# A hybrid layer's delta-rule heads: silu of k in a batch of its own, z projected behind the silu of the rest

## Chip, cores and metric

The kernel runs on one core of a Trainium2 chip. The metric is device microseconds of one execution; three executions of the kernel before are at hand, and one execution has a profile. In the rows PE is TensorE (PEld its weight loads), DVE is VectorE, ACT is ScalarE, POOL is GpSimd and SP is SyncE, which issues most DMAs.

## What is computed

One layer over 1024 tokens and 1024 channels, all in float32. The part that matters here is branch A, eight heads of a bidirectional gated delta rule:

```
h = rmsnorm(x);  proj = h @ w_in                         # q, k, v, z of 8 heads x 128 channels, and more
q, k, v = split(silu(centred_conv5(proj_qkv)))           # convolution of 5 taps along the tokens
q, k = l2norm(q), l2norm(k)
o = delta_rule(q, k, v, decay_f, beta_f) + flip(delta_rule(flip(q, k, v), decay_b, beta_b))
y_a = (rmsnorm(o) * w * silu(z)) @ w_proj_gdn
# branch B: gated linear attention, 4 heads; then gates, a merge, an output projection and a norm
```

## The kernel before

Every product with a weight is made in three matmuls from exact float32r pairs (hi·hi, hi·lo, lo·hi). A block of 128 projected channels (`project`) takes 48 matmuls of 512 columns. Its weight comes in two halves, and each half is loaded by SP (`raw`, two buffers), rounded by ACT (`hi`) and reduced to its rest by POOL (`lo`). `next_w` loads up to four halves ahead of the one that is used. ACT copies the two PSUM banks of a block out: into a padded tile `xp` for k, q and v (three buffers), into `gz` and from there to DRAM (`z_d`) for z.

A head h of branch A goes through these steps:

- `gdn_project`: k, q, v are projected in this order; each is convolved by DVE (five operations of 128x1024, for q the first is ACT's). In the kernel before, the heads from 1 on then project z, load the z of the head before (`zs`, one buffer), and only then run one batch of silu: a load of ACT's silu table, silu of q, k, v and the head before's z, and a load of the table that holds exp and ln. Head 0 has k's silu in a batch of its own already.
- `gdn_decay`: the decays `dt` of 16 units, by small matmuls into the banks `pd`, an exp on ACT (L588) and a mask on POOL (L570).
- `gdn_inverse`: k is transposed into `pk` (L603), ACT copies it and takes its squares, `um` is formed (L629), then inverted: substitution in blocks of 32 on DVE (L652, L654), and blocks of 64 and 128 on PE (L683 to L718). It ends with a ln and an exp on ACT (L724) and the tiles that the scan needs.
- `gdn_scan`: eight steps, both directions side by side, each a chain of PE, DVE and ACT (`r`, `vd`, `vn`, `S`, `po`).

The tiles of q, k, v, `dt`, `um` and `ktok` have two buffers each, so that head h + 2 takes those of head h. The banks of `pd` are those of the scan's `po`.

The order on each engine is made by a planner: every instruction has a place (`cur_priority`), and of those that are ready the one with the lowest place comes first. `gdn_inverse` of the next head stands ahead of `gdn_scan` of this one; projections have the place `P_FILL`, so they fill what the others leave. The result is a fixed queue for each engine. `keep_in_program_order` ties an instruction behind the one emitted just before it on its engine, so the table load of the batch comes behind z's last copy out of PSUM, and each silu behind the one before. Where a queue would run a function whose table is not loaded, a load is put in automatically. The last head has 13 blocks of another projection, the merge gates (`pj_t`), as filling; branch B follows.

Of the kernel before, what the change touches and what calls it, by code (L numbers as in the profile page):

```python
# [14 lines left out]
T = 1024  # L15
# [17 lines left out]
# tiles of loaded weights, of their split parts, of x normalised, of padded projections  # L33
WRAW, WSPLIT, XS, XP = 2, 4, 4, 3
# the order in which a head's k, q and v are projected
A_ORDER = (1, 0, 2)
# the tiles of x that GpSimd scales, the weights whose low parts it takes
X_POOL = (1, 3, 5, 7)
LO_POOL = "azqv"
# blocks of the first projection's gates that are loaded ahead, and the head after whose states  # L40
GA_AHEAD, GA_HEAD = 2, 2
# gates computed beside a head's scan
# [6 lines left out]
# places in the schedule's order  # L49
# [8 lines left out]
def const_array():  # L58
    """Masks and the like: they depend on shapes alone."""
    import numpy as np  # L60

    k = np.arange(P)[:, None]
    i = np.arange(P)[None, :]
    f = lambda m: m.astype(np.float32)
    parts = {}
    parts["ident"] = f(k == i)
    parts["iu"] = f(k <= i)
    parts["il"] = f(k >= i)
    parts["su"] = f(k > i)
    parts["sl"] = f(k < i)  # L70
    cf = np.where(i >= 64, f((k >= 64) & (k <= i)), -f((k > i) & (k <= 63)))
    cb = np.where(i < 64, f((k >= i) & (k <= 63)), -f((k >= 64) & (k < i)))
    lo, hi = f(k <= 63), f(k >= 64)
    parts["cf"] = np.concatenate([cf, lo[:, :1], hi[:, :1]], 1) / 16.0
    parts["cb"] = np.concatenate([cb, hi[:, :1], lo[:, :1]], 1) / 16.0
    p = np.arange(P)
    half = (p % 32) // 16
    r = np.arange(32)[None, :, None]
    s = np.arange(16)[None, None, :]
    parts["yinit"] = f(r == 2 * s + half[:, None, None]).reshape(P, 512)  # L80
    off = 0
    for n, a in parts.items():
        CONSTS[n] = (off, a.shape[1])
        off += a.shape[1]
    return np.ascontiguousarray(np.concatenate(list(parts.values()), 1), dtype=np.float32)
# [3 lines left out]
def layer_kernel(  # L89
# [23 lines left out]
    @contextmanager  # L113
    def at(priority):
        """what is emitted here comes in the schedule's order from this place on"""
        before = tc.cur_priority
        tc.cur_priority = priority
        yield
        tc.cur_priority = before
# [16 lines left out]
    def mm3(ps, lh, ll, rh, rl, n):  # L136
        """ps = (lh + ll)^T (rh + rl), summed over n pieces, without ll^T rl, which is
        below float32's last place."""
        steps = [(a, b, k) for k in range(n) for a, b in ((lh, rh), (lh, rl), (ll, rh))]
        for s, (a, b, k) in enumerate(steps):  # L140
            nc.tensor.matmul(ps, lhsT=a(k), rhs=b(k), start=(s == 0), stop=(s == len(steps) - 1))  # L141

    # ------------------------------------------------------------ what lives throughout
# [16 lines left out]
    # ------------------------------------------------------------ split weights, projections  # L160
    def split(src, hi, lo):
        """src as a float32r pair whose sum is exact"""
        nc.scalar.copy(hi, src)
        nc.vector.tensor_tensor(lo, src, hi.bitcast(F32), op=ALU.subtract)

    def load_w(src, cols, name, g):
        """part of the rows of columns of a weight, [p, k, n], 512 elements of a partition;
        cols: list of (first column, width, place)."""
        n = sum(w for _, w, _ in cols)
        kn = 512 // n  # L170
        raw = wpool.tile([P, kn, n], F32, tag="wraw", name=f"raw_{name}_{g}", bufs=WRAW)
        v = src.rearrange("(k p) n -> p k n", p=P)[:, g * kn:(g + 1) * kn]
        for c, w, to in cols:
            nc.sync.dma_start(raw[:, :, to:to + w], v[:, :, c:c + w])
        hi = wpool.tile([P, kn, n], F32R, tag="whi", name=f"hi_{name}_{g}", bufs=WSPLIT)
        lo = wpool.tile([P, kn, n], F32R, tag="wlo", name=f"lo_{name}_{g}", bufs=WSPLIT)
        i = nc.scalar.copy(hi, raw)  # L177
        if name == "sm":
            tc.keep_in_program_order(i)
        if name[0] in LO_POOL:  # L180
            nc.gpsimd.tensor_tensor(lo, raw, hi.bitcast(F32), op=ALU.subtract)  # L181
        else:
            nc.vector.tensor_tensor(lo, raw, hi.bitcast(F32), op=ALU.subtract)  # L183
        return hi, lo

    # the weights' blocks in the order of their use: parts of them are loaded ahead
# [41 lines left out]
    def project_tokens(name, th, evac):  # L228
        """src^T w for half of the tokens: evac(b, psum) takes [128 tokens, (2 chunks, 256)]"""
        ps = [bank(pj, "pj", f"pj_{name}_{b}") for b in range(2)]  # L230
        for g in range(4):
            hi, lo = next_w(name, g)
            for b in range(2):
                for c in range(2):
                    ts = slice((2 * b + c) * P, (2 * b + c + 1) * P)
                    for k in range(2):
                        kk = 2 * g + k
                        for i, (a, w) in enumerate(((hh, hi), (hl, hi), (hh, lo))):
                            # the first product in a bank clears its marks of what is written
# [6 lines left out]
    def piece(ps, hi, lo, src, th, g, kn, cols=slice(0, 512)):  # L246
        """ps += what the g-th kn pieces of the rows bring, for columns of half of the tokens"""
# [7 lines left out]
    def project(name, evac, src=None):  # L255
        """rows of w^T src: evac(th, psum) takes [channels, 512 tokens]"""
# [8 lines left out]
    def in_steps(name, ps, gn):  # L265
        """as project, by quarters of the tokens"""
# [8 lines left out]
    def project_out(name, dst):  # L275
        """a block of channels kept in DRAM"""
# [13 lines left out]
    # ------------------------------------------------------------ constants of the two mixers  # L290
# [23 lines left out]
    def exp_ln_table():  # L314
        """after a function of another table: the one that has both exp and ln"""
        table(EXP_LN)
# [3 lines left out]
    # ------------------------------------------------------------ h = rmsnorm(x), transposed  # L320
    with tc.tile_pool(name="xpool", bufs=2) as xpool:
# [23 lines left out]
        def scaled(t):  # L345
            """a tile of x normalised, its transpose"""
# [53 lines left out]
    # ------------------------------------------------------------ decays and gates of the scans  # L400
# [6 lines left out]
    def scan_gates(pool):  # L407
# [17 lines left out]
        # [tokens, direction, head, chunk]  # L425
# [19 lines left out]
        # exp of: the sums up to a token, of what is left of the chunk, of the whole chunk  # L445
# [15 lines left out]
    def finish(o_ps, wcol, rs, zs, o, dst, kc):  # L461
        """o * w * rs * zs, to its place in DRAM; zs is overwritten"""
# [5 lines left out]
    def rs_of(sq, pair, lhsT, eps, name, banks):  # L468
        """sq becomes (mean of sq over the channels + eps) ** -0.5; pair: room for sq as a float32r pair"""
# [11 lines left out]
    # ------------------------------------------------------------ gated delta rule  # L481
# [5 lines left out]
    def gdn_project(h, pool):  # L487
        a = [pool.tile([P, T], F32, tag=f"a{j}", name=f"{'qkv'[j]}{h}", bufs=2) for j in range(3)]
        silu = lambda t: tc.keep_in_program_order(nc.scalar.activation(t, t, AF.Silu))
        for j in A_ORDER:  # L490
# [18 lines left out]
            if h == 0 and j == A_ORDER[0]:  # L509
                table(SILU)  # L510
                silu(a[j])
                exp_ln_table()
# [8 lines left out]
        project_out(f"z{h}", z_d[:, h])  # L521
        zs[h - 1] = gdn_z(h - 1, pool)
        table(SILU)
        for t in a + [zs[h - 1]]:
            silu(t)
        exp_ln_table()
        return a
# [3 lines left out]
    def gla_stacks(pool):  # L531
        """(r, 1) and (w2, b2) as float32r pairs, stacked for (r_hi + r_lo)^T (w_hi + w_lo) without
        r_lo^T w_lo, with the other direction's columns zero"""
# [32 lines left out]
    def causal(out, src, d, n):  # L566
        """src where the token of the partition is not after (d = 0) or not before (d = 1)
        that of the column, else 0"""
# [4 lines left out]
    def gdn_decay(h, pool):  # L573
        """dt[j, u, i] = exp(sum of lg over the tokens after j, up to i)"""
# [17 lines left out]
    def gdn_inverse(h, pool, sm, qkv, dt):  # L592
        qT, kT, vT = qkv
        t2 = lambda n, shape: pool.tile(shape, F32, tag="t2", name=f"{n}{h}", bufs=4)
        # keys and values by tokens, norms of the keys
# [22 lines left out]
        # um[j, unit, i] = (k_j . k_i) c1_j dt  # L618
# [13 lines left out]
        # um becomes (1 + um)^-1: blocks of 32 by substitution, all units at once  # L632
# [30 lines left out]
        # forward: yq = y, xq = y^T; backward: the other way round  # L663
# [6 lines left out]
        # blocks of 64, then of 128  # L670
# [55 lines left out]
        # values times the keys' norms, dt times k_j . q_i  # L726
# [17 lines left out]
    def gdn_scan(h, pool, sm, qkv, dt, um, ktok, vtok, c1, c2):  # L744
# [18 lines left out]
        def add_o(n, lhsT, rhs):  # L763
            """the first product in a bank clears its marks of what is written, so that the
            first product in each place writes, and the others add"""
# [45 lines left out]
        # mean of squares over the head's channels, with the norm of q moved under the root  # L811
# [33 lines left out]
    # ------------------------------------------------------------ gated linear attention  # L845
# [6 lines left out]
    def gla_values(h, pool):  # L852
        """values by tokens"""
# [19 lines left out]
    def gla_decay(h, pool, sm, r3, w3):  # L873
        """log decays by tokens (times 16), the directions of a chunk side by side"""
# [15 lines left out]
    def gla_keys(h, pool, sm, gk, qk, cg):  # L890
# [21 lines left out]
        # decay of the state from the middle of a chunk to the middle of the next  # L912
# [24 lines left out]
    def gla_scan(h, pool, sm, o256, vt, gs, qq, kk, cd, ktok, am):  # L937
        # states at the middles of the chunks
# [46 lines left out]
    def gate_a(m, where, tag="ga", bufs=2 * GA_AHEAD):  # L985
        """a block of the first projection's gates"""
# [9 lines left out]
    with tc.tile_pool(name="gla", bufs=1) as pool, tc.tile_pool(name="glas", bufs=2) as sm:  # L996
# [29 lines left out]
        # -------------------------------------------------------- the first output projection  # L1026
        def load_pair(dst, src, pool, tag):
            """src as float32r pairs"""
# [22 lines left out]
    # ------------------------------------------------------------ the second, and the merged  # L1051
# [29 lines left out]
    # ------------------------------------------------------------ out = x + rmsnorm(merged w_out)  # L1081
# [7 lines left out]
    def out_piece(t, c, cols, pool, tag):  # L1089
        """columns of a tile of the output before its norm"""  # L1090
# [14 lines left out]
    # the mean of the squares of the first columns, and eps  # L1105
# [48 lines left out]
```

## Time and profile before

| | us |
|---|---|
| median of 3 executions | 1593.57 |
| lowest, highest | 1586.49, 1595.17 |
| profiled execution: span from its first to its last instruction | 1591.5 |

The page gives no separate device time of the profiled execution; its span lies inside the range of the three and 2.1 us under their median. A row of busy time names engine, share and count; a wait is idle time of an engine just before an instruction, put down to what ended it.

### The profile page before, as it was taken

Reading aid. Unit: us, or ns where it says so; the run is one execution under the profiler, and the core shown is the slowest. Engines: PE = TensorE matmul, PEld = TensorE weight load, DVE = VectorE, ACT = ScalarE, POOL = GpSimd, SP = SyncE. Lnnn points to the kernel's source line nnn. Section 1 sums busy time; section 2 is a strip of 40 time slices with the busy share of each in tenths; the row PEclk is TensorE's granted clock in tenths of the full one; section 3 lists DMA queues with packets and bytes.
Section 4 is the critical chain, followed back from the end, with each engine's and each line's share of the span. In section 5 each row is a group of like instructions: output and inputs, shape, how many; then the busy total and the mean of one; then the engine's idle time right before and its main releaser. Section 6 shows DMA issues by size and latency. Waiting matters only on the chain.

```text
span 1591.5 us, 25255 instructions
## 1 busy us (share of the span) xinstructions
PE 1526.6 (96%) x9622; PEld 1283.3 (81%) x9622; DVE 928.0 (58%) x2467; ACT 673.1 (42%) x1370; POOL 201.8 (13%) x225
## 2 busy tenths in 40 slices
PE   6998999999999999999999999999999999999998
PEld 6877787787878878787778898898888988787887
DVE  5497779979999899887511113314323355445413
ACT  5552535343444545453232325525436355433311
POOL 4242112111112121000000120110100100000000
PEclk9998999999999999998999999999999999999999
DMA  5221102121212121024143331231221335655404
GB/s 168 72 73 34 41 28 86 41 73 35 93 34 71 51 81 47 30 81 133 40 142 94 86 75 38 62 79 34 75 59 41 106 89 190 212 169 175 134 27 157
DMA packets 140882, 133.48 MB, mean 84 GB/s; under 512 B 11147, under 2 KB 114875, under 8 KB 140757
## 3 DMA queue, kind: packets, MB, share of 16 engines
q1 hardware_dynamic: 133282, 117.78, 25.0%
q10 hardware_dynamic: 6840, 12.00, 2.5%
q0 software_dynamic: 640, 2.10, 0.4%
q8 instruction: 75, 1.23, 0.3%
q14 instruction: 45, 0.37, 0.1%
HBM read 101.45 MB, written 30.39 MB: 83 GB/s over the span
## 4 chain that ended last, share of the span: by engine, by line
PE 62%; DVE 11%; DMA 6%; ACT 3%; issue 1%; SPq 1%; ACTq 0%; DVEq 0%
PE pj_t L251 9%; PE pj_y L251 7%; PE pj_v L240 6%; PE pout L141 5%; PE pj_a L251 5%; PE pj_g L251 5%; DVE tmp L652 3%; PE pj_q L251 3%; PE pj_k L251 3%; DVE yl L654 3%; PE pj_z L251 2%; PE po L768 2%; PE psb L946 2%; PE pob L968 2%; PE psc L794 1%; DMA st<-ob_d 1%
## 5 line engine op out<-in xcount | busy, mean ns | idle before, releaser
L251 PE MATMUL pj_a<-hh,hi_a 128*128 128x512 f32 x368 | 151.7, 412 | 0.0
L251 PE MATMUL pj_a<-hl,hi_a 128*128 128x512 f32 x368 | 151.0, 410 | 0.0
L251 PE MATMUL pj_a<-hh,lo_a 128*128 128x512 f32 x368 | 150.5, 409 | 0.0
L251 PE MATMUL pj_t<-hh,hi_t 128*128 128x512 f32 x256 | 103.9, 406 | 2.4 <-ACT gt L281 2.4
L251 PE MATMUL pj_t<-hh,lo_t 128*128 128x512 f32 x256 | 104.4, 408 | 0.0
L251 PE MATMUL pj_t<-hl,hi_t 128*128 128x512 f32 x256 | 104.3, 407 | 0.0
L181 POOL TENSOR_TENSOR lo_a<-raw_a,hi_a 128x512 fp32r<-128x512 f32 x48 | 68.6, 1430 | 235.1 <-ACT hi_a L177 224.9
L789 ACT ACTIVATE vn<-psc,c 128x128 f32<-128x128 f32 x128 | 45.0, 366 | 116.4 <-DVE vd L787 88.8
L652 DVE TENSOR_TENSOR tmp<-ulb,yl 128x54 f32<-128x54 f32 (+13 forms) x480 | 93.3, 235 | 1.3 <-DMA yl<-in_consts_dram 1.2
L654 DVE TENSOR_TENSOR yl<-yl,tmp 128x54 f32<-128x54 f32 (+13 forms) x480 | 90.9, 231 | 0.1
L251 PEld LDWEIGHTS pj_a<-hl,hi_a 128*128 128x128 f32 x368 | 71.1, 193 | 12.6 <-issue 1.0
L251 PEld LDWEIGHTS pj_a<-hh,lo_a 128*128 128x128 f32 x368 | 70.6, 192 | 12.8 <-issue 0.7
L251 PEld LDWEIGHTS pj_a<-hh,hi_a 128*128 128x128 f32 x368 | 70.6, 192 | 12.2 <-issue 0.7
L251 PE MATMUL pj_y<-ob,hi_y 128*128 128x512 f32 x256 | 79.1, 390 | 0.9 <-DVE gb L1073 0.9
L141 PE MATMUL pout<-wo,hh 128*128 128x512 f32 (+1 forms) x272 | 79.7, 377 | 0.0
L240 PE MATMUL pj_v<-lo_v,hh 128*128 128x256 f32 x256 | 72.4, 283 | 0.0
L240 PE MATMUL pj_v<-hi_v,hl 128*128 128x256 f32 x256 | 72.4, 283 | 0.0
L240 PE MATMUL pj_v<-hi_v,hh 128*128 128x256 f32 x256 | 72.4, 283 | 0.0
L181 POOL TENSOR_TENSOR lo_v<-raw_v,hi_v 128x512 fp32r<-128x512 f32 x32 | 41.3, 1290 | 231.9 <-ACT hi_v L177 226.1
L183 DVE TENSOR_TENSOR lo_t<-raw_t,hi_t 128x512 fp32r<-128x512 f32 x32 | 22.0, 689 | 64.1 <-ACT hi_t L177 64.0
L251 PEld LDWEIGHTS pj_t<-hh,hi_t 128*128 128x128 f32 x256 | 49.3, 193 | 12.2 <-ACT gt L281 2.8
L141 PEld LDWEIGHTS pout<-wo,hh 128*128 128x128 f32 x272 | 50.1, 188 | 9.4
(313 smaller groups left out, 4071.3 us busy)
## 6 DMA issues: line engine op xcount, KB each, us to landing
raw_a<-in_w_in_dram SPq DMA_DIRECT2D x48, 256.0 KB
qe<-eg_d SPq DMA_DIRECT2D x16, 512.0 KB
raw_t<-in_w_in_dram SPq DMA_DIRECT2D x32, 256.0 KB
gt_d<-gt SPq DMA_DIRECT2D x64, 128.0 KB
raw_v<-in_w_in_dram SPq DMA_DIRECT2D x32, 256.0 KB
xt<-in_x_dram SPq DMA_DIRECT2D x8, 512.0 KB
raw_z<-in_w_in_dram SPq DMA_DIRECT2D x16, 256.0 KB
z_d<-gz SPq DMA_DIRECT2D x32, 128.0 KB
```

What stands on the lines that cost most here:

```text
L141: nc.tensor.matmul(ps, lhsT=a(k), rhs=b(k), start=(s == 0), stop=(s == len(steps) - 1))
L181: nc.gpsimd.tensor_tensor(lo, raw, hi.bitcast(F32), op=ALU.subtract)
L183: nc.vector.tensor_tensor(lo, raw, hi.bitcast(F32), op=ALU.subtract)
L240: nc.tensor.matmul(ps[b][:, c * 256:(c + 1) * 256], lhsT=a[th][:, kk, ts], rhs=w[:, k, :], start=kk == 0 and i == 0 and c == 0, stop=kk == ...
L251: nc.tensor.matmul(ps[:, cols], lhsT=a[:, k, :], rhs=b[th][:, kk, cols], start=kk == 0 and a is hi and b is src[0], stop=kk == KD - 1 and ...
L652: nc.vector.tensor_tensor(tv, ul2[:, i, 0:i].unsqueeze(2).broadcast_to([P, i, w_]), yv[:, i].unsqueeze(1).broadcast_to([P, i, w_]), op=ALU ...
L654: nc.vector.tensor_tensor(yv[:, 0:i], yv[:, 0:i], tv, op=ALU.subtract)
L768: nc.tensor.matmul(po_n(n), lhsT=lhsT, rhs=rhs, start=count[b] == 1, stop=count[b] == len(todo[b]))
L789: nc.scalar.mul(vn[d], pc[d][:, P:2 * P], c1[:, d, n:n + 1])
L794: nc.tensor.matmul(pc[d][:, 2 * P:3 * P], lhsT=ktok[:, ns], rhs=vd[d], start=True, stop=True)
L946: nc.tensor.matmul(p_s[:, :256], lhsT=ktok[:, u], rhs=vt[:, n], start=True, stop=True)
L968: nc.tensor.matmul(po[e][:, j * P:(j + 1) * P], lhsT=a, rhs=b, start=(i == 0), stop=(i == len(todo) - 1))
```

## The change

Every head now has a silu batch for k alone, directly behind k's convolution. In the heads from 1 on, the second batch takes q, v and the head before's z, and stands directly behind v's convolution; the projection of z is emitted behind it. No buffer, operation or weight order is changed otherwise; comments are dropped.

```diff
             for k in range(1, 5):
                 nc.vector.scalar_tensor_tensor(a[j], xp[:, k:k + T], cw[:, ct, k:k + 1], a[j], op0=ALU.mult, op1=ALU.add)
-            if h == 0 and j == A_ORDER[0]:
+            if j == A_ORDER[0]:
                 table(SILU)
                 silu(a[j])
                 exp_ln_table()
...
-        project_out(f"z{h}", z_d[:, h])
         zs[h - 1] = gdn_z(h - 1, pool)
         table(SILU)
-        for t in a + [zs[h - 1]]:
+        for t in [a[j] for j in A_ORDER[1:]] + [zs[h - 1]]:
             silu(t)
         exp_ln_table()
+        project_out(f"z{h}", z_d[:, h])
         return a
```

## Rows read from the trace of the kernel before

**Rows 1.** The page's part on engines: busy us, share of the span, instructions.

```profile
PE 1526.6 (96%) x9622; PEld 1283.3 (81%) x9622; DVE 928.0 (58%) x2467; ACT 673.1 (42%) x1370; POOL 201.8 (13%) x225
```

**Rows 2.** Stretches: length, busy of PE, PEld, DVE, ACT, POOL, granted clock, DMA.

```profile
60.00:170.00 110.00, 102.24 (x647) 82.69 (x646) 86.29 (x232) 51.61 (x96) 32.66 (x36) 0.94 0.21 61
170.00:700.00 530.00, 505.26 (x3866) 419.55 (x3865) 476.86 (x1494) 241.96 (x528) 92.79 (x111) 0.98 0.18 57
700.00:812.00 112.00, 108.01 (x735) 89.40 (x734) 70.45 (x251) 48.23 (x110) 2.76 (x7) 0.92 0.32 95
812.00:1591.00 779.00, 765.43 (x4057) 649.18 (x4056) 262.08 (x445) 299.31 (x579) 52.38 (x44) 1.00 0.34 101
```

**Rows 3.** What PE waited for, 60 to 812 us: us in total, times, longest.

```profile
PE psc L794 <- ACT vn L789: 11.7, 9, 2.2
PE pd L585 <- DVE xm L583: 8.5, 12, 3.1
PE psc L779 <- DVE S L799: 5.5, 6, 2.2
```

**Rows 4.** The last head's final operation: duration, first and last start.

```profile
L465 DVE SCALAR_TENSOR_TENSOR o<-po,gdn_w,zs x16: 736/743/753, 242.7 to 807.8; 128x512 f32<-128x512 f32 x16
```

**Rows 5.** The chain of waits behind it: start, us, what.

```profile
809.96 6.82 PE pj_t L251 x30
...
824.59 75.35 PE pj_t L251 x324
```

**Rows 6.** ACT in order of time, one head's silu batch.

```profile
432.81 0.66 ACT L281 COPY gz<-pj_z 128x256 f32<-128x256 f32 x2
433.49 1.28 ACT L310 ACT_TABLE_LOAD   x1
...
435.75 1.04 ACT L489 ACTIVATE k<-k 128x1024 f32<-128x1024 f32 x1
```

**Rows 7.** DVE in order of time, k's convolution and um, heads 1 and 4.

```profile
128.81 1.27 DVE L508 SCALAR_TENSOR_TENSOR k<-xp,cw,k 128x1024 f32<-128x1024 f32 x1
...
173.62 1.64 DVE L629 SCALAR_TENSOR_TENSOR um<-pgr,c,dt 128x128 f32<-128x128 f32 x6
...
396.06 1.60 DVE L506 TENSOR_SCALAR k<-xp,cw 128x1024 f32<-128x1024 f32 x1
...
410.57 1.28 DVE L508 SCALAR_TENSOR_TENSOR k<-xp,cw,k 128x1024 f32<-128x1024 f32 x1
...
442.06 4.23 DVE L629 SCALAR_TENSOR_TENSOR um<-pgr,c,dt 128x128 f32<-128x128 f32 x16
```

**Rows 8.** POOL in order of time, the last mask of head 4's decays.

```profile
430.25 0.63 POOL L570 TENSOR_SCALAR_AFFINE_SELECT dt<-dt 128x512 f32<-128x512 f32 x1 [1.43 <-PE psc L779]
```

**Rows 9.** PE in order of time: head 0's inverse; a scan's last read of k.

```profile
143.12 1.00 PE L683 MATMUL p<-xq,um 32*32 32x32 f32 x29 [2.65 <-DVE xq L662]
...
153.42 0.63 PE L251 MATMUL pj_z<-hh,hi_z 128*128 128x512 f32 x1
...
391.62 0.39 PE L251 MATMUL pj_a<-hl,hi_a 128*128 128x512 f32 x1
...
392.54 0.38 PE L779 MATMUL psc<-S,k 128*128 128x128 f32 x2
```

**Rows 10.** SP's queue in order of time, the load of zs.

```profile
411.35 0.42 SPq L563 DMA_DIRECT2D zs<-z_d  x1
```

**Rows 11.** ACT's groups from 60 to 812 us: busy, mean ns, idle before.

```profile
L789 ACT ACTIVATE vn<-psc,c 128x128 f32<-128x128 f32 x128 | 45.0, 366 | 116.4 <-DVE vd L787 88.8 <-PE psc L784 17.4 <-DVE tmp L652 5.9
...
L310 ACT ACT_TABLE_LOAD x19 | 24.4, 1283 | 0.3
```

**Rows 12.** ACT in order of time, head 0's second batch with automatic loads.

```profile
78.23 1.28 ACT L310 ACT_TABLE_LOAD   x1
...
80.60 1.28 ACT L588 ACT_TABLE_LOAD   x1
...
85.92 1.28 ACT L489 ACT_TABLE_LOAD   x1
```

## Prediction

> **What bounds the kernel now.** I began with the page's engine part: PE is busy for 96% of the span, no other engine for more than 58% [rows 1]. The stretches split this. From 812 us on, PE is busy 765 of 779 us at full clock; nothing of the change lies there. The delta-rule heads run from 60 to 812 us. There PE is busy 715.5 of 752 us, so 36.5 us are idle, and the granted clock is 0.94, 0.98 and 0.92. Of its two levels (1.2 and 2.4 GHz) the lower one was granted for some of this time: one minus the clock, times the length, is 6.6 + 10.6 + 9.0 = 26 us lost at most [rows 2]. So PE is the bound in these heads too, and the whole that a better order can win is 36.5 + 26 = 63 us. DVE comes close behind it from 170 to 700 us, with 477 of 530 us.
>
> Next the waits. What PE waits for is the scan (`vn`, `S`) and the products of the decays (`xm`): 25.7 of the 36.5 us in 27 short waits, the longest 3.1 us [rows 3]. None of these names silu or k. They are places where an instruction stands in PE's fixed queue a little before its operand is ready.
>
> The view that decides is the end of the stage. The last operation of the last head starts at 807.8 us [rows 4], and behind it PE still works off gate blocks, 6.8 and 75.4 us of them [rows 5]. These blocks need nothing from the heads. So the heads' own chain has some 82 us of PE work in reserve behind it: if the chain gets 20 us shorter, 20 us more of this filling is left over, and the end stays where it is. The time moves only by what PE idles, or runs at the lower level, more or less than now.
>
> **The change part by part.** *k's silu earlier.* Now the batch's table load follows z's last copy out of PSUM (ends 433.47 us, load at 433.49) [rows 6]. In the shown head the convolution of k ends at 411.85 [rows 7], so z's projection and the batch hold k back for 24 us; in head 1 it ends at 130.1 and `um` starts at 173.62. From the start of k's silu to the start of `um` is 442.06 - 435.75 = 6.3 us [rows 6, 7]; with a table load of 1.28 ahead of it, `um` could start 7.6 us after the convolution: at 419.5 in head 4, at 137.7 in head 1. But `um` also needs the decays, ready at 430.9 in head 4 [rows 8]. So there the gain of the chain is 442.1 - 430.9 = 11 us, and in head 1 up to 36 us. What is late next: the decays, and then the scan, since k's convolution starts (396.06) only behind the last read of the k two heads before (392.54), whose buffer it takes [rows 7, 9]. Buffers and banks do not change, so the 11 us are not gained anew with every head. And all of it is chain, which the 82 us cover; if the cover were gone, 11 us per head would count in full.
>
> What PE itself gains is a smaller sum. In head 0's inverse PE waited 2.65 us and then ran z's matmuls at the lower level (0.63 us for one at 153 us, where 0.39 is usual) [rows 9]; with head 1's inverse beside it some of this may go. Its bounds are 0 and the 63 us; I take 3 us.
>
> *Table loads.* Seven heads get two more explicit loads each, 14 in all. Automatic ones come on top: the load for k is tied only behind the copy of k's projection, and that for the rest only behind v's copy, so ACT can run them long before the convolutions end, and an exp or ln between forces the other table back. Head 0, which has this form already, shows it: load at 78.23, automatic ones at 80.60 and 85.92 [rows 12]. I take 3 automatic loads per head between bounds of 0 and 4, so 35 more loads (14 to 42); at 1283 ns [rows 11] this is 45 us (18 to 54) of ACT, which is busy 342 of 752 us [rows 2]. ACT hides them unless one stands ahead of something that PE is queued for. PE waited 11.7 us for `vn` beside those 342 us of ACT work, 0.034 us per us; 45 us more cost 1.5 us by this, and 45 us if every load were exposed. I take 3, twice the ratio, as the loads fall near the scans.
>
> The load before shows no tail: it starts at 433.49, takes 1.28, and the next function follows at once. The Trainium skill ("ScalarE: Activation LUTs", What ACT_TABLE_LOAD costs) gives about 2.66 us per switch with a drain. By that figure 35 loads would be an estimated 93 us of ACT. The trace does not agree, as 1.28 us is all that the row and the next start leave room for.
>
> *z's projection moved.* It issues 48 matmuls, four copies on ACT, four stores on SP, and with `next_w` two halves of a later weight (two loads on SP, two roundings on ACT, two differences on POOL). In the order of emission it passes one load of `zs` on SP, the table loads and three silus. On PE its place stays behind v and ahead of the next head's k, so no matmul moves past another projection. On SP, the load of `zs` was issued at 411.35, ahead of the batch already [rows 10]. POOL is busy for 93 of 530 us in the middle stretch [rows 2]. Nothing here, so 0; if the roundings fell behind the loads, they would be part of the ACT cost above. The silus themselves are as many as before, so 0 too. Behind a silu that waits for its convolution stand `vn` and the copies out of PSUM in ACT's queue; that cost is the first rival below.
>
> *Sum.* -3 + 3 = 0 on the profiled span of 1591.5, which is 2.1 under the median of the runs shown. Between the two I say 1592.
>
> **The rivals.** *Slower: loads and silus ahead of the scan on ACT.* Scan and batch share ACT; `vn` is on the scan's chain, 16 per head, and is PE's largest wait already [rows 3, 11]. A load that is fully exposed costs 1.28 us, so from one per head on (7 x 1.28 = 9.0 us) the change shows as slower. With two or three per head it is 18 to 27 us: about 1613. Against it: ACT is idle for more than half of the time, and the planner has filling matmuls to put in. The Trainium skill ("ScalarE: Activation LUTs", Rules for kernel authors) says to group functions by table set, which speaks against this change; the price by rows is the one given. Chance 0.25.
>
> *Faster: fewer waits of PE.* The earlier inverse gives the planner more ready work, and short waits and the lower clock behind them go. A quarter to a half of the 63 us is 16 to 31 us: 1576 to 1560, most likely about 1576, since the named waits belong to scans, and the scans do not change. For it: the 36 us in head 1, where DVE has gaps. Chance 0.28.
>
> *The change doesn't do what it says:* the decays or DVE's queue hold `um` where it was, only loads are added, 1592 to 1597. Chance 0.10; it counts with no change. My forecast itself has 0.37.
>
> **How the numbers follow.** A change of 0.5% is 8 us, about what three runs that spread over 8.7 us can tell from nothing. Faster is the second rival's 0.28, no change 0.37 + 0.10 = 0.47, slower 0.25. The range takes in the likely end of both outer cases and leaves their far ends, about 2 in 10, out: 1574 to 1610. The forecast's own range is 1584 to 1600.
>
> **What would show it.** In the new profile, right: 36 to 64 table loads from 60 to 812 us, most likely about 57 (now 22: 19 explicit [rows 11] and the three automatic ones of head 0); k's silu some microseconds behind its convolution; `um` of head 1 some 30 us and of the later heads about 10 us earlier against the last mask of their decays; the last head done before 800 us with more gate blocks behind it; PE idle from 60 to 812 us at 30 to 45 us. Wrong towards slower: PE's wait for `vn` or for copies out of PSUM above 20 us. Wrong towards faster: PE idle under 25 us and a granted clock near 1 from 60 to 170 us and from 700 to 812. The forecast falls if the time from the last head's end on no longer is solid PE work, for then the chain counts.

## The result: 1603.8 us, 0.8% slower

The kernel after takes 1603.76 us (median of 4 runs, 1603.3 to 1606.3); the kernel before took 1591.82 beside it on the same chip. The ratio is 1.0079, interval 1.0057 to 1.0101: slower by more than the 0.5% that the prediction called measurable, and inside its range, but outside the forecast's own 1584 to 1600. The profiled execution's own time was 1604.0 and its span 1602.2, 10.7 us above the span before.

The page's engine part, as in [rows 1]:

```profile
PE 1530.3 (96%) x9622; PEld 1290.7 (81%) x9622; DVE 919.4 (57%) x2467; ACT 720.2 (45%) x1407; POOL 196.6 (12%) x225
```

PE does the same 9622 matmuls; ACT has 37 instructions and 47 us more. The stretches, as in [rows 2], the last one to this span's end:

```profile
60.00:170.00 110.00, 102.30 (x665) 82.58 (x665) 88.12 (x236) 62.06 (x118) 31.57 (x36) 0.97 0.21 61
170.00:700.00 530.00, 504.98 (x3866) 424.39 (x3865) 475.13 (x1562) 283.90 (x561) 88.67 (x111) 0.98 0.18 56
700.00:812.00 112.00, 98.54 (x658) 81.42 (x656) 60.53 (x178) 41.02 (x83) 2.75 (x7) 0.88 0.31 94
812.00:1602.00 790.00, 778.90 (x4115) 659.98 (x4113) 263.05 (x447) 301.07 (x585) 52.41 (x44) 1.00 0.34 100
```

I count PE's loss in a stretch as the prediction counted its 63 us: idle time, plus one minus the granted clock times the length. From 60 to 700 us it is 49.7 us before [rows 2] and 46.6 after; from 700 to 812 us 12.9 before and 13.5 + 13.4 = 26.9 after. The sum grew by 10.9 us and the span by 10.7. (The clock has two digits, which is up to 2.6 us in the stretch of 530 us.) So seven heads cost nothing, and the last head, beside the first gate blocks, lost 14 us.

The waits of PE from 60 to 812 us, as in [rows 3]:

```profile
PE psc L794 <- ACT vn L789: 13.5, 12, 2.7
PE psc L779 <- DVE S L799: 10.6, 12, 2.7
```

PE waits 1.8 us longer for ACT's `vn` than before, where 37 more table loads now stand on ACT (59 in place of 22). ACT's groups, as in [rows 11], explicit loads first and the automatic ones of silu under them:

```profile
L310 ACT ACT_TABLE_LOAD x33 | 42.3, 1283 | 0.6
L489 ACT ACT_TABLE_LOAD x11 | 14.1, 1283 | 0.2
```

The last head's final operation, as in [rows 4], starts 13.2 us earlier than before:

```profile
L465 DVE SCALAR_TENSOR_TENSOR o<-po,gdn_w,zs x16: 737/742/751, 239.9 to 794.6; 128x512 f32<-128x512 f32 x16
```

So the chain did get shorter, and the kernel slower. The chain of waits says why. It is the view of [rows 5], from 745 us on:

```profile
749.79 1.63 SPq L548
751.48 1.96 SPq L549
753.54 1.53 SPq L554
755.63 2.96 DMA qe<-eg_d
...
758.67 0.63 ACT r0h L163
...
759.32 0.04 DVE r0l L164
...
759.93 0.34 DVE r L781
...
774.33 7.88 DMA gt_d<-gt
...
790.81 115.21 PE pj_t L251 x508
```

Before, 82 us of gate blocks stood behind the heads [rows 5]; now it is 115 us in one piece. The chain before that piece runs through SP's queue: branch B's stacked weights (L548 to L554), the last head's `qe`, the split of a stack (`r0h`, `r0l`), and a store of a finished gate block. The blocks did not fill the last head, they waited in it. The same stretch by tile, `pj_t` alone, the first pair being PE's busy time and matmuls:

```profile
700.00:740.00 40.00, 9.49 (x37) 6.47 (x35) 0.00 (x0) 0.79 0.13 39
740.00:785.00 45.00, 14.52 (x48) 8.36 (x47) 2.01 (x6) 0.90 0.30 90
```

The trace of before has 123 and 55 in these stretches, at clocks of 1.00 and 0.81:

```profile
700.00:740.00 40.00, 31.93 (x123) 22.32 (x124) 2.59 (x8) 1.00 0.30 86
740.00:785.00 45.00, 19.15 (x55) 11.18 (x54) 2.02 (x6) 0.81 0.28 83
```

PE in order of time shows two holes in the blocks, 704.65 to 731.63 and 753.07 to 772.72 us, with only the heads' own matmuls in them (in the trace of before no pause of the blocks is as long as 5 us):

```profile
704.65 0.39 PE L251 MATMUL pj_t<-hl,hi_t 128*128 128x512 f32 x1
...
731.63 1.01 PE L251 MATMUL pj_t<-hh,lo_t 128*128 128x512 f32 x1
...
753.07 0.48 PE L251 MATMUL pj_t<-hh,lo_t 128*128 128x512 f32 x1
...
760.33 0.80 PE L784 MATMUL psc<-r,um 128*128 128x128 f32 x2 [4.47 <-DVE r L781]
...
772.72 0.47 PE L251 MATMUL pj_t<-hh,hi_t 128*128 128x512 f32 x1
```

DVE in order of time shows what the first hole waits for. The low part of the blocks' weights, `lo_t`, is made on DVE (`LO_POOL` has no t). One is made at 680.71, and then `um`, the substitution and v's convolution, which waits for its turns, stand ahead of the next. The `hi_t` from which that next one is made was ready on ACT at 683.95 (the first line below), so it stood 39 us in DVE's queue with its inputs there.

```profile
683.33 0.62 ACT L177 CAST hi_t<-raw_t 128x512 fp32r<-128x512 f32 x1 [2.25 <-PE pj_a L251]
```

```profile
680.71 0.64 DVE L183 TENSOR_TENSOR lo_t<-raw_t,hi_t 128x512 fp32r<-128x512 f32 x1
681.56 4.22 DVE L629 SCALAR_TENSOR_TENSOR um<-pgr,c,dt 128x128 f32<-128x128 f32 x16
...
721.87 1.27 DVE L508 SCALAR_TENSOR_TENSOR v<-xp,cw,v 128x1024 f32<-128x1024 f32 x1
723.40 0.68 DVE L183 TENSOR_TENSOR lo_t<-raw_t,hi_t 128x512 fp32r<-128x512 f32 x1
```

In the trace of before a `lo_t` stands between two steps of the same substitution, at 713.90 us. The last 7.5 us of the first hole, from 724.08 to 731.63, are PE's own queue: products of the inverse and a norm of the head before (`pm_a`) stand ahead of the block there.

SP's queue in order of time shows the second hole. No `raw_t` is issued between the pair at 724.10 and 765.54, and the block copied out of PSUM at 741.84 is stored at 762.81. Between them stand the stacks' DMAs, and in the chain above `qe`. The stacks hold up the last head's scan too: `r0l` stands ahead of the scan's `r` on DVE and waits 4.24 us for ACT's `r0h`, and PE waits 4.47 us for that `r` (760.33). The chain view puts the wait of `r0h` down to `qe`'s load, which `r0h` does not read; `r0h` reads the stack's own load of L554, issued just before.

```profile
724.10 6.83 SPq L174 DMA_DIRECT2D raw_t<-in_w_in_dram  x2
...
732.58 4.09 SPq L549 DMA_DIRECT2D w_d<-zero  x4
741.84 4.03 SPq L548 DMA_DIRECT2D w_d<-w2h  x4
...
762.81 1.69 SPq L282 DMA_DIRECT2D gt_d<-gt  x2
765.54 0.39 SPq L174 DMA_DIRECT2D raw_t<-in_w_in_dram  x1
```

### The profile page after: what moved, and what is told of

Its sections match the earlier page's. It is cut to its first block, busy times and chain, and to the rows that moved or that the text cites. A ratio compares the mean times of both kernels' runs of the same rounds, so it can differ in the third digit from the quotient of the medians.

```text
span 1602.2 us, 25317 instructions
## 1 busy us (share of the span) xinstructions
PE 1530.3 (96%) x9622; PEld 1290.7 (81%) x9622; DVE 919.4 (57%) x2467; ACT 720.2 (45%) x1407; POOL 196.6 (12%) x225
## 4 chain that ended last, share of the span: by engine, by line
PE 64%; DVE 11%; DMA 4%; ACT 2%; issue 1%; SPq 0%; DVEq 0%; ACTq 0%
PE pj_t L251 10%; PE pj_y L251 8%; PE pj_v L240 6%; PE pout L141 5%; PE pj_a L251 5%; PE pj_g L251 5%; PE pj_k L251 3%; DVE tmp L652 3%; DVE yl L654 3%; PE pj_q L251 3%; PE po L768 2%; PE pj_z L251 2%; PE psb L946 2%; PE pob L968 2%; DVE xm L583 1%; PE psc L779 1%
## 5 line engine op out<-in xcount | busy, mean ns | idle before, releaser
L794 PE MATMUL psc<-vd,ktok 128*128 128x128 f32 x224 | 46.4, 297 | 13.5 <-ACT vn L789 13.5
L177 ACT CAST hi_a<-raw_a 128x512 fp32r<-128x512 f32 x48 | 29.7, 619 | 62.4 <-issue 30.1
```

Of the source, the lines that this page charges most:

```text
L794: nc.tensor.matmul(pc[d][:, 2 * P:3 * P], lhsT=ktok[:, ns], rhs=vd[d], start=True, stop=True)
```

## The experiments

All are timed against the kernel before on the same chip, whose medians lay between 1588.8 and 1592.0; microseconds of runs on different chips are compared by their ratios. Four theories are named. A: the gate blocks wait for `lo_t` on DVE. B, its rival: the last head's chain and its lower clock lose the time, whoever feeds the blocks. C: the blocks' loads and stores wait in SP's queue. D: the added table loads are the price. "Lost" is counted as above, in the one profiled execution of each. The last column is the number of `pj_t` matmuls from 700 to 740 us. Where a run's heads come earlier or later, these stretches hold other work.

One rival to A to D has no run of its own: that any other order of these queues costs time, whatever its aim. All seven edits that left the kernel before its filling made it slower, by 0.3 to 1.1% (e2, e4, e5, e7, g2, r2, s2), as much as the change. And 13 of the 18 times lay outside every range written ahead (all but e1, e4, e5, n1, n2). So a single time says little here; the holes and waits in the traces, and the same edit made in both kernels, say more.

| kernel | median us | ratio (interval) | lost 60-700 | lost 700-812 | pj_t |
|---|---|---|---|---|---|
| before | | | 49.7 | 12.9 | 123 |
| after | 1603.8 | 1.0079 (1.0057-1.0101) | 46.6 | 26.9 | 37 |
| e1 after, lo_t on GpSimd | 1595.0 | 1.0036 (1.0020-1.0053) | 48.1 | 13.6 | 71 |
| e2 before, lo_t on GpSimd | 1608.3 | 1.0113 (1.0087-1.0139) | 48.6 | 18.7 | 112 |
| e3 after, head 7 as before | 1605.4 | 1.0096 (1.0069-1.0122) | 48.0 | 17.9 | 123 |
| e4 before, change in head 7 | 1593.4 | 1.0029 (1.0003-1.0055) | 48.0 | 14.1 | 101 |
| g1 after, lo_t first | 1599.3 | 1.0054 (1.0040-1.0069) | 47.1 | 20.9 | 80 |
| g2 before, lo_t first | 1596.6 | 1.0036 (1.0021-1.0051) | 46.4 | 9.9 | 106 |
| e6 k's batch alone | 1619.6 | 1.0169 (1.0145-1.0193) | 64.1 | 23.9 | 7 |
| e7 z behind alone | 1597.5 | 1.0039 (1.0019-1.0059) | 52.3 | 11.2 | 94 |
| r1 after, one block's weights | 1601.8 | 1.0078 (1.0048-1.0108) | 44.8 | 22.2 | 31 |
| n1 after, no filling | 1640.6 | 1.0322 (1.0300-1.0344) | 52.4 | 64.2 | 0 |
| n2 before, no filling | 1649.3 | 1.0363 (1.0335-1.0390) | 52.2 | 64.3 | 0 |
| s1 after, stacks at head 4 | 1616.2 | 1.0175 (1.0152-1.0197) | 75.9 | 12.0 | 17 |
| s2 before, stacks at head 4 | 1595.5 | 1.0044 (1.0022-1.0065) | 67.9 | 6.8 | 73 |
| s3 s1 with lo_t first | 1618.9 | 1.0183 (1.0163-1.0203) | 80.5 | 9.7 | 29 |
| e5 loads alone | 1601.0 | 1.0082 (1.0059-1.0106) | 57.6 | 12.9 | 109 |
| q1 after, moves without loads | 1611.4 | 1.0126 (1.0098-1.0154) | 61.3 | 26.0 | 28 |
| u1 g1 with stacks on GpSimd | 1594.5 | 1.0011 (0.9989-1.0032) | 52.4 | 18.1 | 83 |

**The low part of the gates' weights on another engine (e1, e2).**

```diff
-LO_POOL = "azqv"
+LO_POOL = "azqvt"
```

> The changed kernel, with one letter more in LO_POOL: the differences (lo) of the gate weights t come from POOL, not DVE. Theory: the change costs its 11 us in the last head, where the gate blocks that should fill PE wait for lo_t on DVE, which now stands behind the substitution (none from 681 to 723 us); with lo_t on POOL the filling comes back, PE idle from 700 to 812 us falls from 13.5 to under 5 us, and the time falls by 8 to 14 us, to 1590 to 1596. Rival, the extra table loads (36 more) cost it: no change, 1600 to 1606.

> The kernel before with the same one letter in LO_POOL: the control. Theory: there lo_t came in time on DVE, so 1586 to 1594, within 0.4% of the kernel before. If moving lo_t to POOL is a gain by itself, this gains as much as the changed kernel does, 8 us or more, and the first run proves nothing on the change.

In the kernel after this took back 0.4%, some 7 us, and the loss from 700 to 812 us fell from 26.9 to 13.6 us; no hole in the blocks was longer than 6.8 us there, but PE still idled for 10.2 us, where under 5 was expected. In the kernel before the same edit cost 1.1%, against both expectations. POOL in order of time in e2 shows that it changed one queue for another: there are 22 us without a `lo_t`, and in them a clear of the stacks, which waited 12.95 us for a DMA. The last wait of that `lo_t` is for `pj_t`, so the trace does not show that the clear alone held it.

```profile
763.28 1.29 POOL L181 TENSOR_TENSOR lo_t<-raw_t,hi_t 128x512 fp32r<-128x512 f32 x1 [12.75 <-issue]
...
778.64 0.52 POOL L552 MEMSET r<- 64x512 f32 x1 [12.95 <-DMA w_d<-zero]
785.54 1.27 POOL L181 TENSOR_TENSOR lo_t<-raw_t,hi_t 128x512 fp32r<-128x512 f32 x1 [6.38 <-PE pj_t L251]
```

**The change without, and in, the last head (e3, e4).** In both the only difference is whether head 7 has k's own batch and z behind the silu:

```diff
-            if j == A_ORDER[0]:
+            if j == A_ORDER[0] and h < HA - 1:
...
-        project_out(f"z{h}", z_d[:, h])
+        if h < HA - 1:
+            project_out(f"z{h}", z_d[:, h])
```

> The changed kernel, except that the last head (7) has k, q, v and z in one batch behind z's projection, as before. Theory: um of the last head goes back behind v's convolution, lo_t comes in time, 1588 to 1596. Rival, table loads or waits spread over all heads: only one head in seven comes back, 1600 to 1604.

> The kernel before, with the change in the last head (7) alone. Theory: nearly the whole loss, 1598 to 1606, with PE idle above 10 us from 700 to 812 us. Rival, a cost spread over seven heads: a seventh of it, 1591 to 1595.

The theory missed in both. With head 7 as before the kernel stayed at 1605.4, though the blocks were fed (123 matmuls, no hole over 4.8 us). Its last head came later than in the kernel before (`um` at 716.76 in place of 704.79, the last operation at 819.4 in place of 807.8); it lost by a granted clock of 0.89 from 700 to 812 us and, in its trace, some more up to 835 us. With the change in head 7 alone it was 0.3% slower than before, where the rival of a cost spread over the heads had put it; `um` of head 7 started at 696.4, and the longest hole was 7.0 us. So neither the six other heads nor head 7's batch make the two holes by themselves; they come with the whole change. But the six heads alone cost as much time without the holes, by a way that these runs do not show. A cost in every head is not seen in the trace of after: up to 700 us it lost no more than the kernel before.

**lo_t stays on DVE, but first (g1, g2).**

```diff
+        elif name[0] == "t":
+            with at(P_HEAD):
+                nc.vector.tensor_tensor(lo, raw, hi.bitcast(F32), op=ALU.subtract)
```

> The kernel after, with one thing changed: the low part of a gate block's weights (lo_t) stays on VectorE but is given the first place among what is ready there, ahead of the heads' chain. Theory A (the time is lost because the filling waits for lo_t behind the last head's substitution and convolution on VectorE): the holes of 27 and 20 us in the gate blocks go, the loss between 700 us and the first branch-B projection falls from 32 us to about 22, and the time to 1590 to 1597. Rival B (the holes are only what the last head's own chain leaves when it runs, and the loss is in that chain): holes close, but the time stays at 1600 to 1606.

> The kernel before, with lo_t given the first place on VectorE. Theory A: before has no hole to close, so 1587 to 1594. If a reordering beside the last head by itself costs time, whatever its aim, as the move of lo_t to GpSimd cost before 18 us: 1600 to 1610.

g1 closed the 27 us hole to 10.9 and the 20 us one to 6.8, and took back 4 us, less than theory A wanted and between the two spans. g2 cost 0.4% at the median, between its two spans as well, though its profiled execution was one of its fastest (1590.8) and lost less than before.

**Half of the change each (e6, e7).** e6 projects z ahead of the silu again; e7 has one batch of k, q, v and the gate's silu, with z behind it.

> k's silu in a batch of its own, z still projected ahead of the silu of the rest. If the earlier k is what moves the last head against the filling (theory A): 1599 to 1606 with a hole over 15 us in the gate blocks of 690 to 800 us. If z's place is the cause: 1588 to 1595.

> z projected behind the silu, which stays one batch of k, q, v and the gate's silu. Theory A: the inverse starts as before, 1588 to 1595. If z's place is the cause: 1599 to 1606.

k's batch alone is twice as bad as the whole change, outside both of its ranges, with 17 us more lost before 700 us, only 7 gate matmuls between 700 and 740, and a longest hole of 13.7 us; z behind the silu alone costs 0.4%, between its two ranges. So the parts do not add up: behind k's batch, z's move is worth 1.0169 - 1.0079 = 0.9%, some 14 us. No wait by itself carries e6's loss, and why z's place matters so much there stays open.

**No feed at all, or almost (r1, r2).** `project` takes the first block's `hi` and `lo` for all 13:

```diff
-            hi, lo = next_w(name, g)
+            hi, lo = ws[g] if ws else next_w(name, g)
```

> The kernel after, with the 13 gate blocks of the last head all multiplied by the weights of the first of them, which are loaded and split once: 24 loads, high parts and low parts fall away (the gates of the other 12 blocks are then not the reference's; the products, their copies and their stores stay). Theory A (the last head's filling is not fed in time): no hole over 5 us in the gate blocks, the loss after 700 us falls from 32 us to 5 to 15, time 1575 to 1590, and no slower than the same edit of the kernel before. Rival B (the loss lies in the chain of the last head itself): still 8 us or more above the same edit of the kernel before.

> The kernel before with the same edit. Theory A: the loss after 700 us falls from 22 us to 5 to 15, time 1575 to 1588. Rival B: 1585 to 1592, and the kernel after with this edit 8 us or more above it.

r1 took 1601.8 and r2 1595.0 us (ratio 1.0032, 1.0016 to 1.0049): 6.7 us apart, where theory A wanted r1 no slower and rival B 8 us or more. But r1's holes are still there, 702.20 to 727.53 and 749.92 to 767.86 us, for the edit left two ways in which the heads can hold the blocks: the first block's own second `lo_t` (719.38 us on DVE) and the stores, issued on SP at 759.21 behind the stacks. Theory A was too narrow: weights are not the only thing that a gate block needs.

**No filling beside the last head (n1, n2).**

```diff
-GDN_FILL = [0, 0, 0, 0, 0, 0, 0, 13]
-GLA_FILL = [1, 1, 1]
+GDN_FILL = [0, 0, 0, 0, 0, 0, 0, 0]
+GLA_FILL = [5, 5, 6]
```

> The kernel after, with no gate block beside the last head (the 13 blocks are computed beside branch B's heads, 5, 5 and 6 there in place of 1, 1 and 1). The chain of the last head then sets the end of branch A: theory A gives a time below the same edit of the kernel before, by up to the 14 us by which the last scan ended earlier. Rival B: not below it.

> The kernel before with no gate block beside the last head. PE idles beside the last chain, some 45 to 65 us: 1620 to 1660, and by theory A above the kernel after with this edit.

Here the change is a gain: 1640.6 against 1649.3 us, with no overlap of the runs (1640.0 to 1644.5, 1645.0 to 1654.8). The stretches of n1, and then those of n2:

```profile
700.00:800.00 100.00, 73.90 (x521) 59.33 (x519) 57.83 (x189) 32.34 (x62) 5.54 (x8) 0.79 0.16 48
800.00:860.00 60.00, 47.53 (x289) 42.95 (x290) 8.96 (x14) 16.24 (x28) 9.41 (x10) 0.84 0.26 71
```

```profile
700.00:800.00 100.00, 76.18 (x537) 62.53 (x537) 64.39 (x240) 33.22 (x78) 5.98 (x9) 0.74 0.15 46
800.00:860.00 60.00, 41.67 (x248) 35.49 (x247) 10.08 (x14) 20.22 (x32) 8.15 (x9) 0.76 0.22 61
```

With nothing to fill, PE loses 69 us from 700 to 860 us in n1 and 83 us in n2; the shorter chain counts then. This also prices the filling: without it, even the kernel before is 3.6% slower.

**The stacks' place (s1, s2, s3).** `gla_stacks` is emitted at `h == 4` in place of `h == HA - 1`; s3 has g1's edit too.

> The kernel after, with branch B's stacked gate weights (their GpSimd clears and their DMAs on SP's queue) built beside head 4's scan in place of the last head's; nothing else changed. Theory C (the gate blocks' loads and stores stand in SP's in-order queue behind these DMAs and behind the last head's loads): the 20 us hole of 753 to 773 us goes, the earlier one of 27 us stays, the loss after 700 us falls from 32 us to about 22, and the time to 1592 to 1598. Rival B (the loss is in the last head's chain and its lower clock, whoever feeds the blocks): 1600 to 1606.

> The kernel before with the same edit. Theory C: its smaller holes shrink too, 1583 to 1591. If any reordering beside the last head costs time: 1596 to 1605.

> The kernel after with both: the stacks beside head 4 and lo_t first on VectorE. Theory C with A: both holes go, the loss after 700 us falls to 12 to 20 us, 1582 to 1592. Rival B: 1597 to 1606.

Theory C got its last head in part: the loss from 700 to 812 us fell from 26.9 to 12.0 us, and with `lo_t` first to 9.7. In s1 both holes are gone (the longest is 6.1 us), also the first, which was to stay; in s3, where both were to go, one of 15.7 us is there (757.56 to 773.29). All three times missed their ranges. Those of s1 and s3 went up, to 1.0175 and 1.0183, since the loss before 700 us rose by 29 and 34 us; s2 has the same pattern (6 us less, 18 us more). The trace of s1 puts much of it next to head 4 and 5: its granted clock from 530 to 610 us is 0.85, that of after 0.98. That the stacks cost whichever head they stand beside fits this but is not shown: in s2 some 8 of the 18 us are lost from 300 to 420 us, and the first store of the stacks is issued at 499.7.

**The price of the loads (e5, q1).** e5 puts the two explicit loads of k's batch into the kernel before, with no silu between them; q1 takes them out of the kernel after. The automatic loads do not come along: from 60 to 812 us e5 has 36 loads and q1 29, before 22 and after 59.

```diff
-                table(SILU)
-                silu(a[j])
-                exp_ln_table()
+                tc.keep_in_program_order(nc.scalar.activation(a[j], a[j], AF.Identity))
```

> The kernel before with the two table choices put behind k's convolution and no silu there: the loads of the change without its moves. If the loads are free, as the trace of after says (its PE waits for ScalarE's vn grew by 2 us): 1588 to 1595. By the prediction's slower rival, one exposed load of 1.28 us a head: 1596 to 1602.

> The kernel after with k's own batch computed as a plain copy in place of silu, so that its two table loads fall away (k is then not put through silu; the moves of k's batch and of z's projection stay): the moves of the change without its added loads. Theory D (the loads are the whole price, as in the kernel before with the loads alone, 1.0082): 1585 to 1594. Theory B (the moves shift the last head's chain ahead of its filling, and that is where the time goes, loads or not): 1598 to 1606, with the loss after 700 us at 30 us again.

e5 landed on the slower rival's side, 1.0082; read alone it would say that 14 of the 37 loads are the whole loss. q1 says the opposite: the moves with 30 fewer loads cost 1.0126, some 7 us more than with them, above both of its ranges. Its two holes are those of after (717.93 to 746.24 and 767.92 to 786.53 us), and e5 has none over 5.1 us: so the holes belong to the moves and not to the loads. The stretches of q1 show the loss of after in the last head, and another 15 us before 700 us:

```profile
60.00:170.00 110.00, 102.80 (x606) 83.08 (x605) 83.69 (x224) 49.87 (x91) 27.99 (x35) 0.88 0.20 56
170.00:700.00 530.00, 504.98 (x3851) 420.77 (x3850) 471.79 (x1508) 252.71 (x548) 87.95 (x112) 0.97 0.18 57
700.00:812.00 112.00, 99.41 (x671) 81.05 (x671) 71.04 (x241) 43.19 (x86) 2.59 (x5) 0.88 0.25 75
```

PE's wait for `vn` was 7.3 us in e5 and 11.2 in q1, below the 13.5 of after, so in neither is it ACT's queue that PE waits for. A price per load can't be read from these runs: each edit sets the order of all queues anew, and that order moved the time by more than the loads.

**Both holes treated where they are (u1).** g1, with the stacks' DMAs on GpSimd's queue:

```diff
-            nc.sync.dma_start(w2[32 * d:32 * d + 16, :], w[0])
+            nc.gpsimd.dma_start(w2[32 * d:32 * d + 16, :], w[0])
...
-                nc.sync.dma_start(w3_d[d, i, :, :, d], heads(w[rows].bitcast(F32)))
+                nc.gpsimd.dma_start(w3_d[d, i, :, :, d], heads(w[rows].bitcast(F32)))
```

> The kernel after with lo_t first on VectorE (g1, 1.0054) and the DMAs of branch B's stacked gate weights issued on GpSimd's queue in place of SP's; the stacks stay beside the last head, so against g1 only the two queues differ. Theory C (the gate blocks' raw_t loads and gt stores stand behind these DMAs on SP): no hole over 7 us is left in the gate blocks, the loss after 700 us falls from the 25.8 us of g1 to 12 to 20 us, and the time by 6 to 13 us, to 1586 to 1593, level with the kernel before or below it. Rival B (the last head's chain and its lower clock lose the time, whatever the queue): 1596 to 1602, as g1.

1594.5 us, 1.0011 with an interval that holds 1: the loss of the change is gone within the noise, and nothing is won. Two parts of the expectation missed: the time is 1.5 us above its range, and a hole of 10.9 us is left (734.67 to 745.53 us). The kernel before was not run with this edit, so what the queue of the stacks alone is worth is not known. `pj_t` by stretch in u1, against 37 and 48 matmuls in after:

```profile
700.00:740.00 40.00, 22.96 (x83) 15.84 (x83) 1.29 (x4) 0.88 0.24 65
740.00:785.00 45.00, 21.05 (x64) 12.07 (x64) 2.54 (x8) 0.84 0.33 84
```

No version here beats the kernel before.

## Why the prediction was wrong, step by step

**The step that failed** is the view that it called decisive: "These blocks need nothing from the heads. So the heads' own chain has some 82 us of PE work in reserve behind it". The blocks need `lo_t` from DVE, and loads and stores from SP, and both queues are in order and hold the last head's work too. The description ahead of the prediction, by which POOL makes every `lo`, is wrong here: that holds for the projections of k, q, v and z (`LO_POOL`), but the gate blocks' `lo_t` is made on DVE, the engine that the prediction itself found close behind PE. When the last head's inverse moved 23 us ahead (`um` at 681.56, before 704.79), it took DVE from v's convolution and from `lo_t`, and the stacks followed it ahead on SP (their first store at 732.58; in the trace of before at 752.98). The reserve was there to the end, 115 us of it, but could not be drawn on. The trace shows this by the two holes and what stands in the queues. The runs bear it out in part. Against the same edit of the kernel before, the change costs 11.9 us as it is and 2.8 us with `lo_t` first (g1, g2); it gains 13.3 us with `lo_t` on GpSimd (e1, e2) and 8.7 us without filling (n1, n2). With `lo_t` first and the stacks off SP it comes to 1.0011 (u1). Against it stand the pair with the stacks beside head 4, where the change costs 20.7 us (s1, s2), and e3, which loses as much with its blocks fed. So the trace shows that the filling waits in the kernel after; that this waiting, and not just another order of the queues, is the whole price of the change is shown only in part.

**A sign of it that was there:** the prediction asked what the chain waits for, and not what the filling waits for. It also wrote that the forecast falls if the time behind the last head is no longer solid PE work. That test was blind: the time behind it is as solid as before, and the loss lies ahead of it.

**Right:** PE stays the bound. Table loads: about 57 forecast, 59 seen, 1.28 us each. By the trace of after alone their cost is near the 1.5 to 3 us that the prediction gave (PE waits 1.8 us more for `vn` at L794, and 2.2 us at `po`, 4.0 us in all); e5 and q1 neither confirm nor refute a price. The last head was done before 800 us with more blocks behind it. Time up to 700 us unchanged. PE's idle time from 60 to 812 us is 46.2 us, just above the 30 to 45 that were said.

**Head 4's `um`** was to start 11 us earlier, held by the decays. It starts 20.5 us earlier, since the decays came earlier too. ACT, DVE and POOL in order of time, as in [rows 6 to 8]:

```profile
403.73 1.28 ACT L489 ACT_TABLE_LOAD   x1
405.02 1.06 ACT L489 ACTIVATE k<-k 128x1024 f32<-128x1024 f32 x1
```

```profile
421.55 4.22 DVE L629 SCALAR_TENSOR_TENSOR um<-pgr,c,dt 128x128 f32<-128x128 f32 x16
```

```profile
421.78 0.64 POOL L570 TENSOR_SCALAR_AFFINE_SELECT dt<-dt 128x512 f32<-128x512 f32 x1 [1.42 <-ACT dt L588]
```

The mechanism was right: silu starts 3 us behind the convolution, whose last step ends at 402.06, and `um` now starts beside the decays' last mask, where before it came 11 us behind it. But the lead was gained anew: `um` starts earlier by 3.5, 7.5, 7.7, 20.5, 15.4, 19.6 and 23.2 us in heads 1 to 7, where the prediction let the 11 us stand for every head. The 23 us of head 7 are what met the filling.

**Head 1's `um`** was to start some 30 us earlier, and starts 3.5 us earlier (170.10). Its silu did move, to 129.84. PE in order of time shows the next thing that was late, which the prediction did not name:

```profile
161.71 2.05 PE L738 MATMUL pkq<-q,k 128*128 128x128 f32 x16
164.34 0.63 PE L603 MATMUL pk<-call,k 128*128 128x128 f32 x4
```

Head 1's transposes of k follow head 0's inverse, whose last products `pkq` use the same PSUM banks. This is read from the trace; no run tested it.

**z's move at 0** was mis-sized in this setting: a gain of some 14 us by e6 against after. **PE's own gain of 3 us** came out as 3.1 us less loss from 60 to 700 us, no more than the clock's rounding. **The slower rival** named ACT's queue; the time went its way, but PE's waits for ACT did not grow by the 9 us that it asks, and `vn` stayed at 13.5 us, under the 20 that were to show it.

**What stays open:** why e3 loses with its blocks fed, why e5 loses 8 us more up to 700 us than the kernel before, and q1 15 us more than after, and why z's place is worth 14 us. Stretches at a lower granted clock make up a good part of each, and one profiled execution cannot say which of them every execution has. Whether more weight buffers, loaded further ahead, would close the holes was not tried.

## What to carry to other kernels

Work that fills in for a chain is a reserve only if its loads, its conversions and its stores stand in queues that the chain does not hold; follow one filling block through every engine and queue before calling it free. When a chain is made shorter, look at what moves ahead with it into those queues. And where every edit reorders all queues, test a cause by closing the wait itself in both kernels: parts of the change run alone (e5 to e7, q1) did not add up to the whole.

## What the runs showed of the hardware

Issuing a store is not equally short for SP: four stores of the stacks held its queue for 4.09 us (732.58), and the six of this shape in the trace of after took 0.63 to 1.96 us each, where a 256 KB load of `raw_t` took 0.39 us (765.54). So a few of such stores delay what stands behind them on the queue. And a table load took 1283 ns in every group of it seen here, with the function behind it starting at once (403.73 + 1.28, then 405.02).
